# Attention of a two-layer encoder on one core: TensorE issues in source order, and a slot's products run in two halves around its P·V and its transpositions

## The chip, the core and the metric

The kernel runs on 1 core of one Trainium2 chip. The time is the device time of one execution in microseconds (us), and lower is better. Before the change the median of 3 runs is 2469.16 us (2467.95 to 2470.55).

A core has five engines with a queue each: TensorE (PE in the profile: matrix products and transpositions; PEld is its weight loading), VectorE (DVE), ScalarE (ACT), GpSimd (POOL), and SyncE (SP), which here only issues DMAs. The program holds a list of instructions for each engine, and in the trace an engine's instructions start in the order of its list; semaphores hold an instruction back until what it reads is there and what it overwrites has been read.

## What is computed

Two layers, 1040 positions (16 meta tokens and 1024 frames), width 1024. Each layer has a group of gated linear attention heads, a group of 8 heads of softmax attention with a forget-gate bias (the part that the change is about), an output projection and a feed-forward block with a short convolution. The softmax attention, cut to what matters:

```python
c = jnp.cumsum(log_f.astype(jnp.float32), axis=1)
...
logits = jnp.einsum('bqhd,bkhd->bhqk', q_b, kf) + c_b[..., None] - c_k[:, :, None, :]
logits = jnp.where(key_pos[None, :] <= q_pos[:, None], logits, -jnp.inf)
return jnp.einsum('bhqk,bkhd->bqhd', jax.nn.softmax(logits, axis=-1), vf)
```

## The kernel before

Matrix products are done in three terms: each operand is split into a rounded part and a rest (`hi` and `lo` of the weights, `xh` and `xl` of the activations), and `mm3` (L261 to L263) issues hi·xh, lo·xh and hi·xl into one PSUM bank. The split of a weight tile is a ScalarE copy and a subtraction (on GpSimd inside the attention, on VectorE once `self.mixing` is set, in the last part of it).

The softmax attention of a layer is `fox`. Its work is cut into 72 steps: 4 pairs of heads (p), in each pair the query tiles in groups (7,8), (5,6), (3,4), (1,2), (0), in each group the two heads (e), and in each head the one or two tiles of the group (ti, the later tile first). Loop turn n of `fox` is called slot n here; there are 72 + 8 slots, and the last 8 only finish what earlier ones began. For step n, with tile i:

- **Scores**, in slot n (`fox_scores`): 1 to 3 parts of up to 464 keys (3 parts for i = 8 only, 2 for i = 4 to 7, 1 for i < 4). For each part two products into a PSUM bank of the kind `S` (L720 and L721; there are three such banks), then on VectorE the bias and the row minimum (L723, from part to part), then on ScalarE the exponential (L735), which needs the minimum over all parts, writes the tile `P` and frees the bank. There are five `P` buffers (`P_BUFS`); the third part has buffers of its own (`Ps`).
- **T**, in slot n+2 (`fox_transposes`): `P` is transposed in blocks of 116 on TensorE (L756, and L749 for the third part), into one of two banks of the kind `tr`, and for the third part into an `S` bank; a ScalarE copy and a VectorE subtraction split it into `PT` (L377, L378).
- **av**, in slot n+3 of a head's last tile (`fox_av`): P·V for the tiles of the group (L782), into the one bank `av`, then a ScalarE copy to `avs` (L785).
- **fold** and **store**, 4 and 6 slots after the group's last step: transpositions of the result and of its normalised form (L795, L821), both through an `S` bank, with a chain of small VectorE and ScalarE operations between them.

Beside this each slot gets **fill**: `Work.run` takes products of other stages from a queue that `plan` fills. From slots 4, 22 and 40 it holds the q, k and v products of the next pair of heads and then the gate products (`gr_products`: three units of 24 products, each with 6 VectorE and 3 ScalarE operations behind it); from slot 58 the last gate products; from slot 62 the first four tiles of the output projection, whose operands are split on ScalarE and VectorE at that time (`ml`, `mh`). In slots 0 to 3 the queue is empty. Before the change a slot lists av and T of the first part, the scores (at a higher priority), a portion of fill, store, fold, and then av, T and a portion of fill for each further part.

All this is source order. The engines' orders are made from it by a list scheduler, which knows the dependences, reckons with durations of its own and may draw an instruction ahead of earlier ones that would wait; TensorE's order in the attention is its work too. In the feed-forward block TensorE is under `manual_schedule`: there it issues in the order of the source.

## Time and profile before

| what | value |
|---|---|
| median of 3 runs | 2469.16 us |
| the profiled execution's own time | 2467.24 us |
| its span, first to last instruction | 2465.5 us |
| granted TensorE clock, mean | 0.999 |
| TensorE busy | 2437.9 us (99%) |
| VectorE, ScalarE, GpSimd busy | 1876.9 us (76%), 1318.9 us (53%), 384.6 us (16%) |
| softmax attention of layer 0, first score to last store | 166.2 to 500.6 us |
| the same of layer 1 | 1390.5 to 1725.0 us |

A span of 2465.5 us with TensorE busy for 99% of it leaves 27.6 us of idle TensorE. The sum hides two things: matmuls overlap in the profile, so that a busy TensorE is not one at its peak, and the other engines' shares are means over stages that differ much. The two attention stretches are 334.4 and 334.5 us long, 27% of the span together. The profiled execution's own time is 1.74 us above its span and 1.92 us below the median of the three runs.

### The profile page before, as it was taken

To read this page: it belongs to the slowest core of one execution; us is meant where nothing else is said; L and a number is where in the kernel's file an instruction comes from. 1 tells how busy PE (TensorE), PEld (TensorE's weight loads), DVE (VectorE), ACT (ScalarE), POOL (GpSimd) and SP (SyncE) were. 2 spreads that over 40 slices of the span, in tenths; PEclk is the share of its full clock that TensorE was granted. 3 is DMA by queue.
4 is the path that set the end of the run, shared out by engine and by line. 5 is a ranking of instruction groups with operands and counts; after the bars stand their busy time and mean duration, and the time that the engine had idled before them with its cause. 6 is when DMAs were issued, how large, how long until landed. Compare 5 with 4: busy or idle time off the path is not lost.

```text
span 2465.5 us, 47317 instructions
## 1 busy us (share of the span) xinstructions
PE 2437.9 (99%) x18286; PEld 2356.3 (96%) x18286; DVE 1876.9 (76%) x3769; ACT 1318.9 (53%) x2857; POOL 384.6 (16%) x565
## 2 busy tenths in 40 slices
PE   9999999999999999999999999999999999999998
PEld 8999999999999999999999999999999999997887
DVE  8666777769988888865966666777799888887567
ACT  7346666646555555642643566665465555556433
POOL 2023433210000000100210234331100000001002
PEclk9999999999999999999999999999999999999999
DMA  4222224343322214863312222243423212247822
GB/s 135 70 84 76 59 84 132 120 133 95 121 82 74 91 66 144 198 169 124 125 41 73 76 81 74 65 149 106 153 81 108 91 65 91 94 153 172 214 68 88
DMA packets 121680, 260.39 MB, mean 106 GB/s; under 512 B 15248, under 2 KB 37008, under 8 KB 121456
## 3 DMA queue, kind: packets, MB, share of 16 engines
q1 hardware_dynamic: 96864, 182.05, 23.9%
q0 software_dynamic: 22288, 72.81, 10.6%
q8 instruction: 143, 2.34, 0.4%
q10 hardware_dynamic: 2304, 2.52, 0.3%
q14 instruction: 81, 0.66, 0.1%
HBM read 176.74 MB, written 67.80 MB: 99 GB/s over the span
## 4 chain that ended last, share of the span: by engine, by line
PE 68%; issue 16%; DVE 10%; ACT 4%; DMA 1%; POOL 0%; SPq 0%; DVEq 0%; POOLq 0%; ACTq 0%
PE mm L261 8%; PE mm L263 8%; PE mm L262 8%; PE up L262 5%; PE up L263 5%; PE up L261 5%; PE down L262 5%; PE down L263 5%; PE down L261 5%; PE av L782 3%; PE tr L756 2%; PE S L720 1%; DVE S L723 1%; PE S L721 1%; ACT P L735 1%
## 5 line engine op out<-in xcount | busy, mean ns | idle before, releaser
L262 PE MATMUL up<-x,lo 128*128 128x260 f32 x2240 | 631.7, 282 | 1.0 <-DVE lo L1166 1.0
L261 PE MATMUL up<-x,hi 128*128 128x260 f32 x2240 | 631.9, 282 | 0.1
L263 PE MATMUL up<-x,hi 128*128 128x260 f32 x2240 | 631.6, 282 | 0.0
L262 PEld LDWEIGHTS up<-x,lo 128*128 128x128 f32 x2240 | 422.0, 188 | 1.5 <-DVE lo L1166 1.4
L261 PEld LDWEIGHTS up<-x,hi 128*128 128x128 f32 x2240 | 421.7, 188 | 0.4 <-ACT hi L1165 0.3
L263 PEld LDWEIGHTS up<-x,hi 128*128 128x128 f32 x2240 | 421.8, 188 | 0.0
L1165 ACT CAST hi<-raw 128x512 fp32r<-128x512 f32 (+1 forms) x490 | 266.5, 553 | 207.6 <-PE up L263 88.7
L261 PE MATMUL mm<-xh,hi 128*128 128x348 f32 (+6 forms) x1056 | 359.8, 341 | 0.0
L1166 DVE TENSOR_TENSOR lo<-raw,hi 128x512 fp32r<-128x512 f32 (+1 forms) x490 | 288.0, 603 | 79.7 <-ACT hi L1165 79.1
L263 PE MATMUL mm<-xl,hi 128*128 128x348 f32 (+6 forms) x1056 | 339.6, 322 | 0.0
L262 PE MATMUL mm<-xh,lo 128*128 128x348 f32 (+6 forms) x1056 | 338.6, 321 | 0.0
L261 PEld LDWEIGHTS mm<-xh,hi 128*128 128x128 f32 x1056 | 199.4, 189 | 2.3 <-issue 1.4
L262 PEld LDWEIGHTS mm<-xh,lo 128*128 128x128 f32 x1056 | 199.4, 189 | 0.3
L263 PEld LDWEIGHTS mm<-xl,hi 128*128 128x128 f32 x1056 | 198.6, 188 | 0.1
L1147 DVE TENSOR_TENSOR raw<-raw,raw 128x512 f32<-128x512 f32 (+1 forms) x230 | 147.5, 651 | 29.8 <-DMA raw<-in_wd_dram 27.5
L735 ACT ACTIVATE P<-S,m 116x460 f32<-116x460 f32 (+2 forms) x224 | 125.1, 562 | 77.5 <-DVE m L723 74.5
L228 ACT CAST hi<-raw 128x512 fp32r<-128x512 f32 (+2 forms) x152 | 87.4, 576 | 139.6 <-PE mm L263 56.2
L262 PE MATMUL down<-x,lo 128*128 128x260 f32 (+1 forms) x504 | 161.2, 320 | 0.2 <-DVE lo L1166 0.2
L263 PE MATMUL down<-x,hi 128*128 128x260 f32 (+1 forms) x504 | 161.0, 320 | 0.0
L261 PE MATMUL down<-x,hi 128*128 128x260 f32 (+1 forms) x504 | 161.0, 319 | 0.0
L378 DVE TENSOR_TENSOR PT<-tr,PT 116x464 fp32r<-116x464 f32 (+3 forms) x240 | 123.3, 516 | 48.9 <-ACT PT L377 47.2
L1427 POOL DMA_DIRECT2D actd<-cv x44 | 23.6, 537 | 734.6 <-DVE cv L1426 734.6
(313 smaller groups left out, 5957.4 us busy)
## 6 DMA issues: line engine op xcount, KB each, us to landing
raw<-in_wm_dram SPq DMA_DIRECT2D x326, 256.0 KB, 3.1
raw<-in_wd_dram SPq DMA_DIRECT2D x48, 256.0 KB, 4.2
actd<-cv POOLq DMA_DIRECT2D x22, 520.0 KB, 3.0
actd<-cv POOLq DMA_DIRECT2D x22, 512.0 KB, 3.0
cb<-cd SPq DMA_DIRECT2D x16, 520.0 KB, 3.8
kA<-kA SPq DMA_DIRECT2D x24, 260.0 KB, 4.1
kL<-kL SPq DMA_DIRECT2D x24, 260.0 KB, 4.7
st<-actd SPq DMA_DIRECT2D x24, 260.0 KB, 3.8
```

The source lines that it names most:

```text
L228: nc.scalar.copy(hi[:, :n, :], raw[:, :n, :])
L261: nc.tensor.matmul(ps, wh, xh[:, c0:c0 + n], start=first, stop=False, skip_group_check=more)
L262: nc.tensor.matmul(ps, wl, xh[:, c0:c0 + n], start=False, stop=False, skip_group_check=more)
L263: nc.tensor.matmul(ps, wh, xl[:, c0:c0 + n], start=False, stop=last, skip_group_check=more)
L378: nc.vector.tensor_tensor(out=lo, in0=src, in1=hi.bitcast(F32), op=ALU.subtract)
L720: nc.tensor.matmul(S[:rows, :n], q["qA"][e][:, qs], q["kA"][e][:, c0:k1], start=True, stop=False)
L735: nc.scalar.activation(P[:rows, :n], S[:rows, :n], AF.Exp, scale=-1.0, bias=m[:rows, nch - 1:nch], accum_out=(den if nch == 1 else d3[:row ...
L756: nc.tensor.transpose(tr[:w, 3 - j, :rows], P[:rows, o:o + w], id_)
L782: nc.tensor.matmul(av[:, a:b], w.rearrange("p a b -> p (a b)"), x, start=(t == ts[0] and part == 0 and i == 0), stop=(t == last and i == 1))
L1147: nc.vector.tensor_tensor(out=q[out][:, :nk, :], in0=q[a][:, :nk, :], in1=q[b][:, :nk, :], op=op)
L1165: nc.scalar.copy(hi[:, :nk, :], src[:, :nk, :])
L1166: nc.vector.tensor_tensor(out=lo[:, :nk, :], in0=src[:, :nk, :], in1=hi[:, :nk, :].bitcast(F32), op=ALU.subtract)
```

## The change

TensorE is put under `manual_schedule` for the whole of `fox`, so that it issues what the source lists in the order of the source. The other engines are still ordered by the scheduler. The order within a slot is rewritten: scores, half of the slot's fill, av of all parts, T of all parts, fold, store, the other half of the fill.

```diff
@@ fox, the loop over slots
             fill_us = work.left / max(starts[p_next] - n, 1)
-            for kind in ('av0', 'T0'):
-                run(n, kind)
             if n < len(steps):
...
                 self.fox_schedule(lyr, at, n, p, e, ti, i, tiles, Ps, st, qs[p], ap, pp, mix3)
-            parts = [c for c in "12" if (n, "av" + c) in due or (n, "T" + c) in due]
-            work.run(fill_us / (1 + len(parts)))
-            run(n, "store")
-            run(n, "fold")
-            for c in parts:
-                run(n, "av" + c)
-                run(n, "T" + c)
-                work.run(fill_us / (1 + len(parts)))
+            work.run(fill_us / 2)
+            for kind in ("av0", "av1", "av2", "T0", "T1", "T2", "fold", "store"):
+                run(n, kind)
+            work.run(fill_us / 2)
@@ attention
-                self.fox(lyr, ap, pp, qs, plan, lambda: box["mix"][KD - 1])
+                with tc.manual_schedule(engines={mybir.EngineType.PE}):
+                    self.fox(lyr, ap, pp, qs, plan, lambda: box["mix"][KD - 1])
```

No product, transposition or DMA is added or removed. Over a layer's stretch from the first score to the last store TensorE goes over from one kind of work to another (products, scores, av, transpositions) 713 times before and 330 times after in layer 0, and 692 and 330 times in layer 1; it enters a run of transpositions 208 times before and 80 times after in layer 0.

The order on TensorE at the start of a layer's attention, before: behind the scores of slot 0 stand eighteen products of the fill (`mm`), of which the last is the first row here, then the scores of slot 1 (`S` with `kA_1594`), the first of slot 2 (`kA_1595`, the other head), and T of slot 0's step among them.

```order
L263 MATMUL mm<-xl_146,hi 128x344
L720 MATMUL S<-kA_1594,qA_1592 116x460
L721 MATMUL S<-kL_1596,qA_1592 116x460
L756 MATMUL tr<-ident,P 116x116 x2
L720 MATMUL S<-kA_1594,qA_1592 116x464
L721 MATMUL S<-kL_1596,qA_1592 116x464
L720 MATMUL S<-kA_1595,qA_1593 116x460
L721 MATMUL S<-kL_1597,qA_1593 116x460
L756 MATMUL tr<-ident,P 116x116 x6
L261 MATMUL mm<-xh_147,hi 128x344
L262 MATMUL mm<-xh_147,lo 128x344
L263 MATMUL mm<-xl_148,hi 128x344
```

The same place after: the first row is the first score of slot 1, which stands right behind those of slot 0.

```order
L720 MATMUL S<-kA_1594,qA_1592 116x460
L721 MATMUL S<-kL_1596,qA_1592 116x460
L720 MATMUL S<-kA_1594,qA_1592 116x464
L721 MATMUL S<-kL_1596,qA_1592 116x464
L720 MATMUL S<-kA_1595,qA_1593 116x460
L721 MATMUL S<-kL_1597,qA_1593 116x460
L720 MATMUL S<-kA_1595,qA_1593 116x464
L721 MATMUL S<-kL_1597,qA_1593 116x464
L720 MATMUL S<-kA_1595,qA_1593 116x116
L721 MATMUL S<-kL_1597,qA_1593 116x116
L756 MATMUL tr<-ident,P 116x116 x8
L749 MATMUL tr<-ident,Ps 116x116
```

What moved: the products are gone from between the scores of slots 0 to 3; the first now stand behind the scores of slot 4. T of a step stands in one run behind all scores of its slot.

The order on TensorE in slot 20, before: scores of the second head's tile 8 (three parts), with av of tile 0 of the pair before (`PT_3267`) and T of slot 18's step among them.

```order
L795 MATMUL fo<-ident,avs 116x128 x4
L782 MATMUL av<-PT_3267,V_1599 128x112
L720 MATMUL S<-kA_2327,qA_2325 116x460
L782 MATMUL av<-PT_3267,V_1599 128x112
L721 MATMUL S<-kL_2329,qA_2325 116x460
L756 MATMUL tr<-ident,P 116x116
L720 MATMUL S<-kA_2327,qA_2325 116x464
L756 MATMUL tr<-ident,P 116x116
L721 MATMUL S<-kL_2329,qA_2325 116x464
L756 MATMUL tr<-ident,P 116x116 x2
L720 MATMUL S<-kA_2327,qA_2325 116x116
L721 MATMUL S<-kL_2329,qA_2325 116x116
```

The same slot after, from the last products before its scores to the second product behind them; nine products stand between these scores and the slot's av, T and T of the third part (`Ps`).

```order
L262 MATMUL mm<-xh_143,lo 128x348
L263 MATMUL mm<-xl_144,hi 128x348
L720 MATMUL S<-kA_2329,qA_2327 116x460
L721 MATMUL S<-kL_2331,qA_2327 116x460
L720 MATMUL S<-kA_2329,qA_2327 116x464
L721 MATMUL S<-kL_2331,qA_2327 116x464
L720 MATMUL S<-kA_2329,qA_2327 116x116
L721 MATMUL S<-kL_2331,qA_2327 116x116
L261 MATMUL mm<-xh_145,hi 128x348
L262 MATMUL mm<-xh_145,lo 128x348
```

What moved: before, another kind of work stands between the scores of most parts; after, the three parts come at once, and whatever one of them waits for holds all that is listed behind it.

The order on VectorE from slot 19's first score part to slot 20's, after (`L687` to `L691` are the gate operations of the fill, `den` the sum of a row's exponentials, `ff` the copy that frees the fold's bank):

```order
L687 TENSOR_TENSOR gog<-gx,gog 128x344
L378 TENSOR_TENSOR V_2333<-tr,V_2333 116x2x64
L723 ISA S,m<-S,cb,m 116x464
L723 ISA m 116x1
L378 TENSOR_TENSOR Vm<-tr,Vm 116x64
L688 SCALAR_TENSOR_TENSOR ge<-ge,gy 128x344
L378 TENSOR_TENSOR PT_3295<-tr,PT_3295 112x112
L689 SCALAR_TENSOR_TENSOR gy<-ge,gy 128x344
L691 SCALAR_TENSOR_TENSOR gog<-gy,gog 128x344
L739 TENSOR_REDUCE den<-d_3273 116x1
L799 TENSOR_TENSOR ff<-fo,ff 116x256
L723 ISA S,m<-S,cb 116x460
```

Before, the same operations stand here in nearly the same order; VectorE's list changes little, and what changes is when TensorE delivers to it.

## The prediction, made before the changed kernel was run

> **What bounds the kernel now.** I read the page first, then windows over the two attention stretches, then the timelines of TensorE, ScalarE and VectorE at the places where the windows show idle TensorE. The page's span and TensorE's row:
>
> ```profile
> span 2465.5 us, 47317 instructions
> PE 2437.9 (99%) x18286; PEld 2356.3 (96%) x18286; DVE 1876.9 (76%) x3769; ACT 1318.9 (53%) x2857; POOL 384.6 (16%) x565
> ```
>
> TensorE bounds the kernel. The change moves work on TensorE alone, within the softmax attention, so the question is how much idle it removes there or makes. The windows (microseconds busy per engine, instructions in brackets) are the start of layer 0's attention, the scores of tiles 8 and 7 of the second and of the fourth pair of heads, and the turn to the output projection:
>
> ```profile
> core 0: us, PE busy (x) PEld busy (x) DVE busy (x) ACT busy (x) POOL busy (x), PEclk, DMA share, GB/s
> 166.00:186.00 20.00, 18.64 (x120) 15.61 (x119) 14.69 (x49) 13.93 (x43) 5.30 (x8) 1.00 0.15 46
> 245.00:265.00 20.00, 19.68 (x137) 18.12 (x136) 19.11 (x63) 15.88 (x50) 6.44 (x9) 1.00 0.22 69
> 405.00:425.00 20.00, 19.57 (x131) 17.87 (x130) 18.14 (x63) 17.29 (x55) 5.12 (x10) 1.00 0.34 118
> 445.00:463.00 18.00, 14.88 (x112) 13.79 (x111) 17.86 (x54) 14.88 (x43) 5.74 (x11) 1.00 0.48 136
> ```
>
> The reader should see VectorE: busy for 19.11 of 20 us and 18.14 of 20 us in the tile-8 zones and 17.86 of 18 us at the turn. TensorE keeps up there only because what it is given next is mostly ready. An order that makes VectorE idle in these zones lengthens them. At the start neither VectorE nor ScalarE is full, but TensorE has fill to do: rows of its timeline there (start, duration, line, shape, count).
>
> ```profile
> 167.62 0.21 PE L720 MATMUL S<-kA,qA 128*116 128x116 f32 x1
> 167.68 0.26 PE L721 MATMUL S<-kL,qA 128*116 128x116 f32 x1
> 167.78 0.38 PE L261 MATMUL mm<-xh,hi 128*128 128x344 f32 x1
> 167.99 0.32 PE L262 MATMUL mm<-xh,lo 128*128 128x344 f32 x1
> 168.15 0.32 PE L263 MATMUL mm<-xl,hi 128*128 128x344 f32 x1
> ...
> 170.77 0.47 PE L720 MATMUL S<-kA,qA 128*116 128x460 f32 x1
> ...
> 182.18 0.40 PE L782 MATMUL av<-PT,V 116*128 116x256 f32 x2
> 182.42 0.56 PE L756 MATMUL tr<-ident,P 116*116 116x116 f32 x4
> 182.74 0.41 PE L782 MATMUL av<-PT,Vm 116*128 116x116 f32 x2
> ...
> 184.46 0.26 PE L756 MATMUL tr<-ident,P 116*116 116x116 f32 x1
> 184.48 0.36 PE L720 MATMUL S<-kA,qA 128*116 128x232 f32 x1
> 184.68 0.27 PE L721 MATMUL S<-kL,qA 128*116 128x232 f32 x1
> 184.78 0.32 PE L263 MATMUL mm<-xl,hi 128*128 128x348 f32 x1
> ```
>
> **Part 1, fewer changes of kind: a saving.** What counts is the distance between starts. The lone transposition at 184.46 gives way after 0.02 us, but the score behind it then takes 0.20 instead of the 0.10 of its twin at 184.68: 0.12 together, and the four at 182.42 cost 0.08 each plus about 0.1 once behind them, 0.10 to 0.11 each. A run thus costs some 0.013 us of its own, and 128 of 208 runs per layer go: 1.7 us. The narrow score at 167.62 leaves after 0.06 since its twin uses the same weights; the twin leaves after 0.10, and the product behind it after 0.21 instead of 0.16: 0.1 us lost where a narrow matmul meets other weights. I count about 78 such places per layer in the order before and 51 after: at most 3 us. The saving is 1.7 to 4.8 us per layer; some of the narrow ones cost only half, so I take 4.0. Parts 2 to 4 compare whole stretches, which have their share of it within them, 92 of a layer's 334.4 us; outside them 2.9 us are left, with the ends 1.7 and 3.5.
>
> **Part 2, the start: a loss.** Slots 0 to 3 have no fill, and it now stays behind slot 4's scores. ScalarE and VectorE rows there:
>
> ```profile
> 169.99 0.64 ACT L735 ACTIVATE P<-S,m 116x460 f32<-116x460 f32 x1 [0.21 <-DVE m L723]
> ...
> 170.71 0.66 ACT L735 ACTIVATE P<-S,m 116x464 f32<-116x464 f32 x1
> ...
> 172.85 0.55 ACT L377 CAST PT<-tr 116x464 fp32r<-116x464 f32 x1 [1.04 <-PE tr L756]
> ```
>
> ```profile
> 171.49 0.65 DVE L723 CUSTOM_DVE_ANT_0 S<-S,cb 116x460 f32<-116x460 f32 x1 [0.41 <-PE S L721]
> ...
> 172.37 0.71 DVE L723 CUSTOM_DVE_ANT_0 S<-S,cb,m 116x464 f32<-116x464 f32 x1 [0.17 <-DVE den L739]
> ...
> 173.59 0.64 DVE L378 TENSOR_TENSOR PT<-tr,PT 116x464 fp32r<-116x464 f32 x1
> ```
>
> Three S banks carry all scores, so slot 1's first part waits for the exponential of slot 0's, done at 170.6: before, eighteen products fill 167.78 to 170.77, and after, TensorE stands for 2.99 us. From there I follow the new order with these durations (a minimum 0.65 to 0.75, an exponential 0.65, a cast of PT 0.55, its subtraction 0.64, a wide score pair 0.42). Slot 2's second part needs slot 1's exponentials, which begin after its second minimum at 172.9: it starts at 173.6 (1.4 us idle), its third at 174.2. T of slot 0 runs to 175.1; its third block needs the bank of slot 2's first part, whose minimum ends at 175.0 and exponential at 176.0 (0.95 idle). Slot 3's scores wait for slot 2's further exponentials (0.6), T of slot 1 for the casts and subtractions of the T before it (0.6), slot 4's second part for slot 3's exponential, queued on ScalarE behind two casts, until 179.8 (0.8). At 180.2 the fill begins; some 7.4 us were idle. Before, TensorE had finished slot 5's scores at 184.78. After, it still owes at 180.2 the 32 products done by then (at 0.157, 5.0 us), av of the first pair of tiles (16 at 0.12 and two narrow ones, 2.1 us), 13 transpositions (1.3) and slot 5's scores (0.6): 189.2. The loss is 4.4 us per layer; 3.4 if ScalarE's list takes an exponential before a cast at one place more, 5.4 if each hop between engines costs 0.1 us more than I reckon.
>
> A page of the Trainium skill speaks against this change here: "TensorE: Matmul & The Clock Gate", section "Part 1: The HAM clock gate", says that after an idle window of about 3.4 us the array's clock falls to half until it has been busy for as long. No run here shows it: the granted clock is 1.00 in every window above. By the page the sum would hardly change for 2.99 us of idle, and the rival below prices the other case.
>
> **Part 3, three zones per layer: a loss.** Slots 18 to 21, 36 to 39 and 54 to 57 hold tiles 8 and 7 and, at the same time, the gate units with their six VectorE operations each. Rows of VectorE in the first zone (gate, `den`, slot 19's first part, the end of the gate chain, slot 20's first part) and of TensorE (first scores of slots 18, 20 and 22):
>
> ```profile
> 242.41 0.52 DVE L680 TENSOR_TENSOR gx<-mm,r 128x344 f32<-128x344 f32 x1 [0.80 <-PE mm L263]
> 243.38 0.16 DVE L739 TENSOR_REDUCE den<-d 116x1 f32<-116x3 f32 x1 [0.45 <-ACT Ps L735]
> ...
> 244.32 0.64 DVE L723 CUSTOM_DVE_ANT_0 S<-S,cb 116x460 f32<-116x460 f32 x1
> ...
> 247.25 0.50 DVE L691 SCALAR_TENSOR_TENSOR gog<-gy,gog 128x344 f32<-128x344 f32 x1
> ...
> 248.11 0.64 DVE L723 CUSTOM_DVE_ANT_0 S<-S,cb 116x460 f32<-116x460 f32 x1
> ```
>
> ```profile
> 238.64 0.42 PE L720 MATMUL S<-kA,qA 128*116 128x460 f32 x1
> ...
> 246.78 0.47 PE L720 MATMUL S<-kA,qA 128*116 128x460 f32 x1
> ...
> 257.95 0.38 PE L720 MATMUL S<-kA,qA 128*116 128x460 f32 x1
> ```
>
> Before, slots 18 to 22 take 19.3 us. In the new order I count from slot 18's first score. TensorE reaches slot 20 after 8.35 us; but VectorE, idle from 2.5 to 4.3 us until slot 18's exponentials let `den` pass, takes slot 19's second minimum only at 7.5 to 8.3, the exponential that frees the bank ends at 9.15, and the third bank (the fold's) is read by VectorE until 10.55: 1.45 us idle, as the three parts now stand in one block. T's third block, listed behind slot 20's av and T, waits 0.55 for slot 20's first exponential (13.7). That is 2.0 us. In slot 21 the two T wait 0.6 each for the tr banks, since the subtractions stand behind gate operations on VectorE, the fold 0.25 for the bank of T's third block, and the store 1.2 for slot 21's exponential, whose second minimum is last in VectorE's row: 2.65 more, if all stand. Slot 22 then begins at 22.5, or at 19.85 with slot 20's waits alone. Before it began at 19.3 with 0.7 us of its av done, so at 18.6 for the same work. The zone costs 1.25 to 3.9 us more. The idle of slot 20 itself gives VectorE time to catch up, so I take a third of slot 21's part (0.9): some 2.2, times three, 6.6 per layer, ends 3.75 and 11.7.
>
> **Part 4, the turn to the output projection.** What it waits for there (us in total over both layers, times, longest):
>
> ```profile
> PE tr L756 <- DVE PT L378: 3.7, 5, 1.4
> PE mm L263 <- DVE ml L378: 2.1, 2, 1.0
> ```
>
> VectorE is full either way. The wait of 1.0 for `ml` goes, because av and T now stand ahead of those products. In its place the second unit waits for its weights' subtraction, 2.1 us by VectorE's list, and later av waits some 2 us for PT behind seven splits of `ml`, where before nine further products covered it. Against TensorE's 3.1 us of idle in this window I take 1.0 us more per layer, ends 0 and 2.
>
> DMAs keep their places: each is issued by SP or GpSimd, whose lists follow the scheduler as before, and none stands on TensorE's waits above except weights fetched a tile ahead. Outside these places every operand of a slot is made one or two slots earlier (334.4 / 80 = 4.2 us each), which covers a cast and a subtraction (1.2 us) and two minima with their exponentials (2.7 us); without that cover each part of scores would cost its chain.
>
> **The sum.** Per layer −2.9 + 4.4 + 6.6 + 1.0 = +9.1 us, for two layers +18.2. Against the profiled execution's own time of 2467.24 that is 2485.4; against the median of 2469.16, 1.92 higher, 2487.4. The low ends give −3.5 + 3.4 + 3.75 + 0 = +3.65 per layer, 2476.5; the high ends −1.7 + 5.4 + 11.7 + 2 = +17.4, 2504.0.
>
> **Rivals.**
> - *The banks are free in time, and the regrouping pays: faster.* Scores that come in one block give VectorE its minima earlier. If each exponential then ends before its bank is wanted, the zones keep no wait at all (slot 22 at 17.85 instead of 18.6, −0.75 each), the turn costs nothing, and of the start only the empty slots' first 2.99 us and the 1.4 us behind them stay, 4.4 of its 7.4 us idle, a loss of 1.4: −2.9 + 1.4 − 2.25 = −3.75 per layer, 2461.7. For it: ScalarE has 4 us of room in the zone. Against it: VectorE's 19.11 of 20. It decides at exponentials 0.8 us earlier than mine in slot 19.
> - *The start alone costs:* the zones' and the turn's waits vanish, the start stays at 4.4: −2.9 + 4.4 − 2.25 = −0.75 per layer, 2467.7, no change that can be told. Zones at 0.9 us each and the turn at 0 give +4.2 per layer; between these, up to +2.4 per layer, lies the case "same".
> - *TensorE is slow for a while after the start's idle.* At half speed the 5.0 us of its work in slots 1 to 4 take 5.0 more, of which the waits there hide all but some 1.7 us: +3.4 for both layers, 2490.8. The Trainium skill's page cited in part 2 has this rule. For it: 7.4 of 12.4 us idle, with 2.99 in one piece; against it: a longest idle of 1.4 us is all that before shows, at clock 1.00.
>
> **How the numbers follow.** Forecast 0.67, the clock's case 0.05, the start alone 0.17, the regrouping pays 0.11. The forecast's own range is 2474 to 2504; to hold 8 in 10 I let the range begin at 2469, within the case of no change, and end at 2503. No change means within 0.2% (4.9 us), about what a measurement of this kernel can tell: slower 0.72, same 0.17, faster 0.11.
>
> **What would show it.** In the profile after: at both starts a first score idle by about 3 us behind ACT P, and TensorE busy some 13 of 20 us; in each zone idle before L720 and L749 behind ACT P and before L756 behind DVE PT, VectorE below its 19.11; an attention stretch longer by 9 us per layer; feed-forward stretches unchanged. I would be wrong if the zones' waits are absent (2.5 us or less per layer), or if waits appear in slots 6 to 17, which I hold covered.

## The result: slower by 46 us, two and a half times the forecast

| | before | after |
|---|---|---|
| median of six runs | 2469.69 us (2467.95 to 2471.59) | 2515.68 us (2510.45 to 2520.04) |
| ratio | | 1.0183, 95% interval 1.0173 to 1.0194 |
| span of the profiled execution | 2465.5 us | 2511.6 us |
| softmax attention of layer 0, first score to last store | 334.4 us | 352.0 us (166.80 to 518.75) |
| the same of layer 1 | 334.5 us | 359.7 us (1411.72 to 1771.43) |

The sign was forecast; the size (+18.2, range to 2503) was not. The two stretches are longer by 17.6 and 25.2 us, 42.8 of the 46.1 us between the two spans. Of the other 3.3 us, 3.1 lie between the two stretches; about 1 us of that is products that moved out of the first one (below), and the rest is not explained here.

The page after the change: span, TensorE's row, and the clock in 40 slices.

```profile
span 2511.6 us, 47351 instructions
PE 2453.9 (98%) x18286; PEld 2366.3 (94%) x18286; DVE 1885.7 (75%) x3769; ACT 1320.8 (53%) x2857; POOL 386.9 (15%) x565
...
PEclk9999999999999999999999899999999999999999
```

The same 18,286 matmuls make TensorE "busy" for 16.0 us more than before, and one slice of the clock has an 8: some of the busy time is slow time. The windows (columns as before: busy us per engine, PEclk is the granted clock) of the start, two zones and the turn of layer 0, and the start and third zone of layer 1:

```profile
166.00:186.00 20.00, 14.63 (x65) 10.80 (x64) 12.45 (x42) 10.83 (x34) 3.42 (x6) 0.74 0.17 50
248.00:269.00 21.00, 18.06 (x115) 15.63 (x114) 16.95 (x57) 14.74 (x49) 5.44 (x9) 1.00 0.21 67
418.00:439.00 21.00, 17.14 (x110) 14.77 (x109) 16.00 (x55) 15.64 (x51) 5.44 (x12) 1.00 0.45 148
460.00:478.00 18.00, 13.58 (x104) 12.59 (x103) 17.89 (x50) 14.12 (x42) 5.53 (x10) 1.00 0.35 108
...
1411.00:1435.00 24.00, 18.64 (x92) 14.66 (x92) 12.53 (x43) 12.17 (x39) 3.42 (x6) 0.72 0.14 40
...
1665.00:1693.00 28.00, 22.90 (x123) 20.75 (x123) 17.96 (x62) 16.57 (x52) 6.59 (x13) 0.82 0.40 131
```

At the start TensorE starts 65 matmuls in 20 us where it started 120. In the first and third zone of layer 0 VectorE has fallen from 19.11 and 18.14 of 20 us to 16.95 and 16.00 of 21: no engine is full there any more, they wait for each other. What TensorE waits for (us over both layers, times, longest), and one row of VectorE:

```profile
PE S L720 <- ACT P L735: 15.4, 14, 3.2
PE tr L756 <- DVE PT L378: 6.7, 14, 0.8
PE tr L821 <- ACT P L735: 6.2, 6, 1.1
...
DVE S L723 <- POOL cb L894: 4.1, 2, 2.8
...
PE mm L262 <- DVE wl L230: 3.5, 2, 1.8
PE av L782 <- DVE PT L378: 3.3, 2, 1.7
...
PE mm L263 <- DVE ml L378: 2.1, 2, 1.1
```

Before, the first of these rows was:

```profile
PE S L720 <- ACT P L735: 1.9, 4, 0.6
```

and no wait ahead of the store (L821) was long enough to be listed. To see where the time went, the stretches are cut at the first scores of certain slots. From each piece's length I subtract what its matmuls take at full rate, by distances between starts in undisturbed rows: 0.417 ns per column plus 13 ns for a product, 99 ns per 116 columns for a transposition. What is left is the piece's overhead, in us; it holds waits, slow starts and, where the clock is low, the slower streaming:

| piece (slots) | before, layer 0 / 1 | after, layer 0 / 1 | difference |
|---|---|---|---|
| start (0 to 5) | 3.28 / 3.34 | 11.22 / 12.01 | +7.94 / +8.67 |
| 5 to 17 | 2.27 / 2.22 | 2.18 / 2.13 | −0.09 / −0.09 |
| first zone (17 to 22) | 2.09 / 1.81 | 5.43 / 5.41 | +3.34 / +3.60 |
| 22 to 35 | 1.93 / 2.45 | 1.25 / 1.23 | −0.68 / −1.22 |
| second zone (35 to 40) | 1.87 / 1.81 | 5.41 / 6.79 | +3.54 / +4.98 |
| 40 to 53 | 1.86 / 2.39 | 1.31 / 2.60 | −0.55 / +0.21 |
| third zone (53 to 58) | 2.32 / 2.07 | 6.29 / 11.20 | +3.97 / +9.13 |
| 58 to 62 | 0.54 / 0.84 | 0.34 / 0.37 | −0.20 / −0.47 |
| turn (62 to 67) | 4.61 / 4.57 | 5.81 / 5.79 | +1.20 / +1.22 |
| 67 to the last store | 1.08 / 1.04 | 1.25 / 1.21 | +0.17 / +0.17 |

Together +18.6 and +26.2: the starts 16.6, the six zones 28.6, the turns 2.4, and −2.8 for the rest, where the regrouping was to pay. (Some 1 us of products per layer left the stretch and stands behind its end, so that the stretches are longer by 42.8 and not by 44.8.)

### The profile page after: what moved, and what is told of

The parts are those of the page before. It is cut to its first block, busy times and chain, and to the rows that moved or that the text cites. A ratio compares the mean times of both kernels' runs of the same rounds, so it can differ in the third digit from the quotient of the medians.

```text
span 2511.6 us, 47351 instructions
## 1 busy us (share of the span) xinstructions
PE 2453.9 (98%) x18286; PEld 2366.3 (94%) x18286; DVE 1885.7 (75%) x3769; ACT 1320.8 (53%) x2857; POOL 386.9 (15%) x565
## 4 chain that ended last, share of the span: by engine, by line
PE 50%; issue 31%; DVE 12%; ACT 3%; DMA 3%; POOL 1%; SPq 0%; POOLq 0%; DVEq 0%; ACTq 0%
PE mm L261 7%; PE mm L262 7%; PE mm L263 7%; PE down L261 5%; PE down L262 5%; PE down L263 5%; PE av L782 3%; PE tr L756 2%; PE S L720 1%; PE S L721 1%; DVE S L723 1%; DVE x L1186 1%; PE wo L263 1%; PE wo L262 1%; PE wo L261 1%
## 5 line engine op out<-in xcount | busy, mean ns | idle before, releaser
L378 DVE TENSOR_TENSOR PT<-tr,PT 116x464 fp32r<-116x464 f32 (+3 forms) x240 | 117.5, 514 | 65.3 <-ACT PT L377 64.5
```

The lines of the kernel that those rows point to most:

```text
L378: nc.vector.tensor_tensor(out=lo, in0=src, in1=hi.bitcast(F32), op=ALU.subtract)
```

## The experiments

### Which part of the change costs

The new source order alone, without `manual_schedule`:

```diff
-                with tc.manual_schedule(engines={mybir.EngineType.PE}):
-                    self.fox(lyr, ap, pp, qs, plan, lambda: box["mix"][KD - 1])
+                self.fox(lyr, ap, pp, qs, plan, lambda: box["mix"][KD - 1])
```

> One part of the change alone: the new source order within a slot, with TensorE's order left to the list scheduler. Theory: the loss comes from TensorE being held to the source's order at places where the scheduler would have drawn products forward (slots 0 to 3, and the zones of tiles 8 and 7). Then this kernel is near the one before: 2465 to 2478, no window of granted clock 0.50 in the attention, TensorE idle at the starts no more than the kernel before. Rival: the regrouping itself costs, whoever orders TensorE; then 2495 or more.

2479.21 us, ratio to before 1.0024 to 1.0054. (Each group of runs has its own median of the kernel before, 2468.7 to 2469.4 us, and the ratios go by that.) The starts (3.12 and 4.59, of which 1.2 us in layer 1 is a wait for a DMA) and zones (1.71 to 2.43) are those of the kernel before or near; what it loses, it loses in the quiet slots (4.04 and 3.04 in 22 to 35, 4.02 and 3.06 in 40 to 53), where scores wait for exponentials. It is 1.2 us over the upper end of the expectation, and one window of 3.41 us at clock 0.50 stands at layer 1's turn, where none was expected.

`manual_schedule` alone, with the old order within a slot:

```diff
-                self.fox(lyr, ap, pp, qs, plan, lambda: box["mix"][KD - 1])
+                with tc.manual_schedule(engines={mybir.EngineType.PE}):
+                    self.fox(lyr, ap, pp, qs, plan, lambda: box["mix"][KD - 1])
```

> The other part alone: TensorE in source order, with the old source order within a slot (av and T of the first part, scores, fill, store, fold, av and T of further parts with fill between). Theory: the start stays as bad as in the changed kernel (slots 0 to 3 hold no products, 8 us per layer, clock at 0.50 there), but the zones lose less since products stand between the runs of transpositions: 2480 to 2500. Rival: the old order, made for a scheduler, waits in every slot once it is held, since av and T stand ahead of the scores: over 2515.

2491.93 us, 1.0077 to 1.0107, as expected: starts 9.24 and 10.00, zones 2.77 to 3.97, and turns 8.24 and 5.87, in layer 0 with 6.83 us at clock 0.50. So the parts cost 9.8 and 22.6 us alone and 46.0 together. Holding TensorE to the source costs the start with either order; the zones' large waits need both parts.

### The start: missing fill, and a clock that matters less than it shows

The products of the next pair queued from slot 0:

```diff
-        starts = [f + 4 for f in first] + [first[3] + 8, len(steps) + 8]
+        starts = [0] + [f + 4 for f in first[1:]] + [first[3] + 8, len(steps) + 8]
```

> The changed kernel with the products of the next pair queued from slot 0 instead of slot 4, so that slots 0 to 3 have fill. By the trace of the changed kernel the stretch from slot 0 to slot 5 costs 7.9 us in layer 0 and 8.7 us in layer 1 more than before. Theory: all of it is the missing fill (waits and, behind them, the clock at 0.50 for 10.2 and 13.7 us), so 2515.7 - 16.6 = 2499, within 2496 to 2503, and clock 1.00 at both starts. Rival: only the waits that the prediction counted go (4.4 us per layer) and the rest moves to slots 4 to 17, whose fill gets thinner: 2505 to 2510.

2499.59 us, 1.0106 to 1.0140; 16.1 less than the changed kernel, as expected. Starts 4.30 and 3.50, clock 1.00:

```profile
166.00:190.00 24.00, 21.67 (x142) 19.38 (x141) 13.49 (x44) 13.97 (x43) 8.38 (x11) 1.00 0.13 40
```

The changed kernel has 98 matmuls in this window and a clock of 0.79 (its row stands below). Is the clock the cause or a companion? Two kernels add products that nobody reads, where TensorE waits:

```diff
+    def keep(self, pp, q, n):
+        ps = pp.tile([128, 512], F32, tag="mm", name="keep")
+        for i in range(n):
+            self.nc.tensor.matmul(ps[:, :348], q["qA"][0][:, 0:128], q["kA"][0][:, 0:348], start=i == 0, stop=i == n - 1)
...
+            if n in (0, 1, 2, 3):
+                self.keep(pp, qs[0], 8)
             work.run(fill_us / 2)
             for kind in ("av0", "av1", "av2", "T0", "T1", "T2", "fold", "store"):
                 run(n, kind)
+                if n in (21, 39, 57) and kind in ("T1", "fold"):
+                    self.keep(pp, qs[p], 3)
```

> The changed kernel with extra products whose result is never read, put where TensorE waits: eight of 348 columns behind the scores of slots 0 to 3, and three behind the transpositions and behind the fold of slots 21, 39 and 57. They change no wait of the work itself; they only keep TensorE active. Clock theory: the clock falls to 0.50 at the end of a 3.41 us window in which TensorE streams less than about 1 us (transpositions counted half). Then it stays at 1.00 at both starts and in the zones, except perhaps ahead of slot 56 of layer 1, where TensorE waits 3.2 us with nothing added. In the changed kernel some 24 us of streaming lie in the slow windows, which at full speed take 12 less: 2503 to 2509 with the waits unchanged, so that the waits are the larger part of the loss. Rival: the low clock only fills time in which TensorE would have waited anyway: 2513 to 2520.

2507.90 us, 1.0141 to 1.0172: 7.8 less. Both starts are at clock 1.00, yet slot 5 begins 22.8 and 22.3 us after the first score, against 23.2 and 24.0 (17.7 and 17.8 before). The start of layer 1:

```profile
1411.00:1435.00 24.00, 21.65 (x136) 18.57 (x137) 14.50 (x50) 12.35 (x41) 3.47 (x7) 1.00 0.11 37
```

One fall was left, in slot 56 of layer 1, and one came at that layer's turn. Since in slots 2 and 3 the eight products might take more time than the waits there, the second kernel has 8, 5, 2 and 2 of them:

```diff
+                self.keep(pp, qs[0], (8, 5, 2, 2)[n])
```

> The changed kernel with extra products whose result is never read, as before in the zones (three behind the transpositions and three behind the fold of slots 21, 39 and 57), and fewer at the start: 8, 5, 2 and 2 behind the scores of slots 0 to 3, which is what fits into the waits of 2.9, 1.3 and 0.5 us there; with eight in each slot they stood in the way themselves (1.3 us of them in slots 2 and 3 were not covered). Theory: the clock stays at 1.00 and slot 5 begins 20.5 to 21.5 us after the first score instead of 23.2 and 24.0 (17.7 before the change): about 2.5 us per layer are the clock's, 3 to 4 the waits'. The total: 2503 to 2506. Rival: the chain of minima, exponentials, casts and subtractions alone makes 22.5 us or more: 2506 to 2509.

2508.96 us, 1.0143 to 1.0171. In layer 0 the clock holds (in layer 1 it fell for 6.8 us at the start once more), and slot 5 begins 22.9 us after the first score. The rival holds. The windows of this kernel and of the changed one:

```profile
166.00:190.00 24.00, 18.97 (x116) 15.25 (x115) 13.39 (x45) 12.84 (x40) 3.42 (x6) 1.00 0.14 42
```

```profile
166.00:190.00 24.00, 18.63 (x98) 14.80 (x97) 13.19 (x45) 12.87 (x40) 3.42 (x6) 0.79 0.14 42
```

The same row but for the extra products and the clock. The second product of the first scores waited 0.56 us longer for a DMA here than in the changed kernel (0.68 against 0.12), so the clock is worth 0.3 to 0.9 us in layer 0. In layer 1 keep_all begins slot 5 1.74 us earlier, but the changed kernel also waits 0.42 us longer there for the same DMA, so that 1.3 to 1.7 us are the clock's. At half speed TensorE mostly fills time in which it would have waited for ScalarE and VectorE.

### The zones: four waits in one run

All that follow but the last are built on the kernel with fill from slot 0. The table gives their zones' overheads in us, first, second and third of each layer; the names are those of the experiments below. The times are medians, the overheads those of the profiled execution. For fill from slot 0 this one took 2495.57 us, 4.0 less than the median of its four, so that gains against its row come out low; in it the clock fell for 3.41 us in each zone of layer 1.

| kernel | us | layer 0 | layer 1 |
|---|---|---|---|
| before | 2469.7 | 2.09, 1.87, 2.32 | 1.81, 1.81, 2.07 |
| fill from slot 0 | 2499.6 | 6.14, 5.40, 6.66 | 7.10, 6.76, 8.95 |
| mid_fill | 2492.8 | 6.97, 3.65, 6.65 | 8.03, 3.43, 6.74 |
| gate_light | 2488.2 | 6.11, 3.97, 6.55 | 6.11, 4.00, 9.07 |
| gate_moved | 2508.9 | 7.18, 8.83, 7.11 | 8.46, 8.79, 7.02 |
| cb_act | 2496.0 | 7.26, 6.69, 5.08 | 6.17, 6.78, 5.44 |
| store_av | 2494.6 | 6.16, 4.18, 6.01 | 7.34, 4.16, 6.49 |
| t0_first | 2492.0 | 4.48, 3.99, 4.79 | 4.42, 3.97, 4.68 |
| old_fill_manual | 2481.6 | 4.34, 2.80, 3.12 | 4.36, 2.87, 3.82 |

Slot 21 of the changed kernel on TensorE (start, duration, shape, count; in brackets the idle time ahead and what ended it):

```profile
263.03 0.32 PE L263 MATMUL mm<-xl,hi 128*128 128x348 f32 x1
263.82 0.58 PE L756 MATMUL tr<-ident,P 116*116 116x116 f32 x4 [0.47 <-DVE PT L378]
264.80 0.58 PE L756 MATMUL tr<-ident,P 116*116 116x116 f32 x4 [0.40 <-DVE PT L378]
265.85 0.43 PE L795 MATMUL fo<-ident,avs 128*112 128x128 f32 x2 [0.47 <-DVE PT L378]
267.30 0.42 PE L821 MATMUL tr<-ident,fon 116*128 116x116 f32 x2 [1.01 <-ACT P L735]
267.48 0.41 PE L261 MATMUL mm<-xh,hi 128*128 128x348 f32 x1
```

and on VectorE in the same time:

```profile
262.03 0.65 DVE L723 CUSTOM_DVE_ANT_0 S<-S,cb 116x460 f32<-116x460 f32 x1 [1.10 <-PE S L721]
...
262.60 0.52 DVE L688 SCALAR_TENSOR_TENSOR ge<-ge,gy 128x348 f32<-128x348 f32 x1
263.04 0.63 DVE L378 TENSOR_TENSOR PT<-tr,PT 116x464 fp32r<-116x464 f32 x1
263.59 0.51 DVE L689 SCALAR_TENSOR_TENSOR gy<-ge,gy 128x348 f32<-128x348 f32 x1
264.02 0.63 DVE L378 TENSOR_TENSOR PT<-tr,PT 116x464 fp32r<-116x464 f32 x1
264.57 1.04 DVE L691 SCALAR_TENSOR_TENSOR gog<-gy,gog 128x348 f32<-128x348 f32 x1
265.53 0.27 DVE L378 TENSOR_TENSOR PT<-tr,PT 116x116 fp32r<-116x116 f32 x1
265.72 0.69 DVE L723 CUSTOM_DVE_ANT_0 S<-S,cb,m 116x464 f32<-116x464 f32 x1
```

Four groups of transpositions wait in a row, 2.35 us, with nothing between them. VectorE, idle until the slot's first scores come, then takes gate operations and subtractions in turn, and the slot's second minimum last; the exponential that frees the store's S bank comes behind that minimum. In the kernel with fill from slot 0 the second and third zones wait in the same way; in the first zones the two T wait 1.8 us, and the store does not.

A third of the fill between T and fold:

```diff
-            work.run(fill_us / 2)
-            for kind in ("av0", "av1", "av2", "T0", "T1", "T2", "fold", "store"):
-                run(n, kind)
-            work.run(fill_us / 2)
+            work.run(fill_us / 3)
+            for kind in ("av0", "av1", "av2", "T0", "T1", "T2"):
+                run(n, kind)
+            work.run(fill_us / 3)
+            for kind in ("fold", "store"):
+                run(n, kind)
+            work.run(fill_us / 3)
```

> On top of the kernel with fill from slot 0 (2499.6): the fill of a slot in thirds, scores, a third, av and T, a third, fold and store, a third. What is left of the loss there lies in the three zones of a layer (slots 17 to 22, 35 to 40, 53 to 58), 11.9 us in layer 0 and 17.1 us in layer 1 above the kernel before. Theory: the store of slot 21 (1.0 us behind the exponential of the same slot's scores) and the fold wait because they stand right behind the transpositions; five products ahead of them cover 0.8 of it, and no window without products is left, so the clock stays at 1.00: 6 times 1.2 and some 3 for the clock, 2487 to 2493. Rival: the waits are VectorE's backlog and only move to the next slot: 2497 to 2501.

2492.75 us, 1.0080 to 1.0110, within the range, but not in the way expected: the second zones gain 1.8 and 3.3, the first lose 0.8 and 0.9, slots 22 to 35 lose 1.2 and 0.5, and the store still waits 6.3 us in all. The clock fell seven times in the attention.

Two of the gate's VectorE operations left out:

```diff
-            nc.vector.scalar_tensor_tensor(out=e, in0=e, scalar=1.0, in1=y, op0=ALU.add, op1=ALU.mult)
-            nc.vector.scalar_tensor_tensor(out=y, in0=e, scalar=-2.0, in1=y, op0=ALU.add, op1=ALU.mult)
```

> On top of the kernel with fill from slot 0: two of the gate's six VectorE operations are left out (L688 and L689, so the gate's value is another one); the products, the DMAs and ScalarE's part stay. Theory of the prediction (step 3): in slot 21 the subtractions of PT and the second minimum stand behind the gate's operations on VectorE, 0.5 us each, so the zone's waits shrink by 0.5 to 1.0 us: 6 zones, 2493 to 2497. Rival: the waits are the chain transposition, cast, subtraction, bank itself, whatever VectorE does beside it: 2498 to 2501.

2488.22 us, 1.0063 to 1.0097: 11.4 less, more than expected, 3.6 of it at the turns (3.93 and 4.03 instead of 5.77 and 5.81), where gate operations also stand. TensorE's wait for PT ahead of T falls from 7.1 us (13 times) to 1.4 (3 times), but the store's rises from 4.2 to 6.7 us, and the scores' wait for the fold's bank (`ff`) from 0.4 to 3.4: the first wait of the row is shortened and later ones take much of it back. Only the second zones (1.4 and 2.8 us) and the first of layer 1 (1.0) gain, and in these two of layer 1 a fall of the clock is gone as well.

The gate's products moved ahead of the v products:

```diff
                         self.gr_products(lyr, p, w, ap, pp, nm)
+                        w.q[6:] = w.q[9:] + w.q[6:9]
+                        w.boxes[2:] = w.boxes[:1:-1]
@@ fox
             work.run(fill_us / 2)
+            if n in starts[1:4]:
+                self.flush()
             for kind in ("av0", "av1", "av2", "T0", "T1", "T2", "fold", "store"):
```

> On top of the kernel with fill from slot 0: in the first three plans the gate's products are queued behind the k products instead of behind the v products, so that the gate's VectorE work lies in slots 12 to 17 (light tiles) and the v products, with about half of that work, in the zone. All of the computation stays. Theory: the zones wait since the gate's operations stand on VectorE among those of tiles 8 and 7; then the zones lose some 2 us less each and the clock does not fall: 2483 to 2491. Rival: av of slot 22 then waits for V (its last products now end there), and the zone only changes its wait: 2496 to 2504.

2508.93 us, 1.0146 to 1.0176: 9.3 worse than its base, against both expectations. Slot 21 has no wait now, as the theory says of the gate, in any of the six zones, but the v products' own transpositions take the `tr` banks of the zone:

```profile
255.60 0.58 PE L756 MATMUL tr<-ident,P 116*116 116x116 f32 x4 [1.94 <-DVE V L378]
...
258.88 0.96 PE L756 MATMUL tr<-ident,P 116*116 116x116 f32 x8
259.68 0.38 PE L795 MATMUL fo<-ident,avs 128*112 128x128 f32 x2
260.18 0.42 PE L821 MATMUL tr<-ident,fon 116*128 116x116 f32 x2
```

The third zone has one more cause, which the prediction had excluded. Rows of layer 0, changed kernel, by engine (SPq is SyncE's queue):

```profile
409.38 0.33 SPq L869 DMA_DIRECT2D cb<-cd  x1
417.06 0.34 SPq L219 DMA_DIRECT2D raw<-in_wm_dram  x1
417.44 0.42 SPq L869 DMA_DIRECT2D cb<-cd  x1
```

```profile
415.74 1.29 POOL L230 TENSOR_TENSOR lo<-raw,hi 128x512 fp32r<-128x512 f32 x1
...
423.80 0.82 POOL L894 TENSOR_TENSOR cb<-cb,mask 116x116 f32<-116x116 f32 x2 [5.17 <-DMA cb<-cd]
```

```profile
424.66 0.71 DVE L723 CUSTOM_DVE_ANT_0 S<-S,cb,m 116x464 f32<-116x464 f32 x1 [1.23 <-POOL cb L894]
```

```profile
426.25 0.47 PE L720 MATMUL S<-kA,qA 128*116 128x460 f32 x1 [1.87 <-ACT P L735]
```

The new order of the other engines' lists put a weight DMA between the bias rows (`cb`) of a pair's two heads on SyncE. It waits for its buffer, which GpSimd's split of an earlier tile frees at 417.03, and the second row comes 8.06 us after the first (2.32 before the change; over the six zones 5.6 to 8.1 against 2.3 to 3.6). GpSimd, in its own order, waits for that row ahead of a mask that the first head needs, VectorE for the mask, ScalarE and TensorE behind it. In layer 1 TensorE waits 3.18 us there. First try, the mask written later in the source:

```diff
-                        self.fox_mask(cbs[p][x], NT - 1)
+                if g == 0 and ti == 1:
+                    self.fox_mask(cbs[p][e], NT - 1)
```

> On top of the kernel with fill from slot 0: the first mask on the second head's bias row (cb) is written in the source at the second head's first scores (slot 20, 38, 56) instead of the first head's (slot 18, 36, 54). In the changed kernel the DMA of that row stands on SyncE behind a weight DMA and comes 4.9 to 7.6 us after the first row's (0.4 to 3.6 us before the change's kernel), and GpSimd, in its own order, waits for it ahead of the first head's next mask; in the third zone VectorE's minimum of slot 55 then waits 1.2 us in layer 0 and 2.8 us in layer 1 for that mask, and TensorE's scores of slot 56 1.9 and 3.2 us. Theory: without that order the wait ahead of slot 56 shrinks to the 0.5 us of the other zones, 1.3 and 2.6 us less and one clock window less: 2494 to 2497. Rival: the row itself is late for the second head, and the wait moves to slot 56: 2498 to 2501.

2498.39 us, 1.0105 to 1.0136. VectorE still waits 3.7 us for the mask: the scheduler placed GpSimd's masks as before, and the run tells nothing on the cause. (The delays of the row quoted in its expectation were misread; those above are the rows'.) Second try, the second row through another queue:

```diff
-                        nc.sync.dma_start(cbs[p][x][:, :T],
+                        (nc.scalar if x else nc.sync).dma_start(cbs[p][x][:, :T],
```

> On top of the kernel with fill from slot 0 (2499.6): the bias row (cb) of a pair's second head is fetched through ScalarE's queue, so that it no longer stands behind a waiting weight DMA on SyncE. Writing its mask later in the source (the run before) left GpSimd's order as it was and told nothing. Theory: the 1.2 and 2.2 to 2.8 us that VectorE's minimum in the third zone waits for GpSimd's mask go, and with them 1.3 us of the zone in layer 0 and 2.5 to 4 us in layer 1 (a window of the clock too): 2494 to 2496. Rival: the wait there is VectorE's own backlog and stays: 2498 to 2501.

2495.99 us, 1.0092 to 1.0126: VectorE's wait for the mask is gone from the list, the third zones lose 1.6 and 3.5 us less, as expected. In the first two zones of layer 0 the clock fell instead, 1.1 and 1.3 us.

The store in the bank of av:

```diff
-        tr = pp.tile([128, 4, 128], F32, tag="S", name="tr")
-        trf = tr[:].rearrange("p a b -> p (a b)")
+        trf = pp.tile([128, 256], F32, tag="av", name="tr")
```

> On top of the kernel with fill from slot 0 (2499.6): the store's transpositions go to the bank of av (no av stands in slots 21, 39 and 57) instead of an S bank. Theory: of the zone's waits the store's 1.0 to 1.1 us in slot 21 is that for an S bank, behind an exponential whose minimum is last in VectorE's row; it goes in four to six zones, and a clock window or two with it: 2492 to 2496. Rival: fold and store are also late by their own chain, or av of the next slot waits for the store's bank: 2498 to 2501.

2494.60 us, 1.0080 to 1.0110. The store follows the fold without a wait:

```profile
1585.50 0.43 PE L795 MATMUL fo<-ident,avs 128*112 128x128 f32 x2 [0.47 <-DVE PT L378]
1585.77 0.36 PE L820 MATMUL tr<-ident,fon 116*128 116x116 f32 x2
```

The second and third zones gain 6.9 us together (in the first the store had no wait in this base); the turns lose 4.8, where av now waits for the store's bank, and layer 0's start lost 2.4 more, with a wait of 1.9 us for a DMA and a fall of the clock. So the store's wait is one for the bank.

T and av of the first part ahead of the scores, all else new:

```diff
+            for kind in ("av0", "T0"):
+                run(n, kind)
             if n < len(steps):
...
-            for kind in ("av0", "av1", "av2", "T0", "T1", "T2", "fold", "store"):
+            for kind in ("av1", "av2", "T1", "T2", "fold", "store"):
```

> On top of the kernel with fill from slot 0 (2499.6): in a slot, av and T of the first part stand ahead of the scores, as the kernel before lists them; all else keeps the new order. What is left of the loss is in the zones, 4.0, 3.5, 4.3 us in layer 0 and 5.3, 5.0, 6.9 us in layer 1 above the kernel before; with TensorE in the old order these were 0.7, 0.9, 0.8 and 1.1, 1.0, 1.9. Theory: two T of a slot right behind each other need both tr banks at once, and each waits for the other's cast and subtraction; with the scores and half of the fill (2.6 us) between them the wait goes: 2482 to 2490. Rival: the store, which waits 1.0 us for an S bank, is the larger part, or a T ahead of the scores only delays these: 2495 or more.

2492.02 us, 1.0079 to 1.0109, between the two expectations. All six zones shrink, by 1.4 to 4.3 us, and no clock falls in them. The waits for PT are gone from slots 21, 39 and 57, as the theory says; what is left in the zones are T's third block (1.3 to 1.4 us) and the store (1.0 to 1.2). But slots 22 to 35 (2.78) and the turns (8.72 and 8.63 instead of 5.8, with 6.83 us at clock 0.50 in each) give about half of it back.

The old order held, with fill from slot 0 (the kernel of the second run with the one line that gave the changed kernel its fill):

```diff
-        starts = [f + 4 for f in first] + [first[3] + 8, len(steps) + 8]
+        starts = [0] + [f + 4 for f in first[1:]] + [first[3] + 8, len(steps) + 8]
```

> TensorE in source order, the old order within a slot, and fill from slot 0. The kernel with the old order held (2491.9) loses 6.0 and 6.7 us more than the kernel before from slot 0 to slot 5, 4 us in its zones and 3.6 and 1.3 us at the turn to the output projection. Theory: fill at the start takes away 5 to 6.5 us per layer as it did with the new order (6.9 and 8.5), the rest stays: 2479 to 2483. Rival: T ahead of the scores waits for its P at the start whatever fill there is: 2486 or more.

2481.55 us, 1.0033 to 1.0063, as expected. The difference to the same with the new order, 18 us, is what the new order costs once TensorE is held: zones of 5.4 to 9.0 instead of 2.8 to 4.4, while the old order loses 2.8 us more at the turns.

### Is there a version that gains?

Fill from slot 0 in the kernel before, by the same line:

```diff
+        starts = [0] + [f + 4 for f in first[1:]] + [first[3] + 8, len(steps) + 8]
```

> The kernel before (2469.3) with fill from slot 0 and nothing else; the list scheduler orders TensorE. Theory: the scheduler drew products forward into slots 0 to 3 anyway (2.2 us of lag there beyond that of other slots), so at most 1 us per layer is to be had: 2467 to 2470. Rival: the fill of slots 4 to 17 gets thinner and the scores wait there: 2471 to 2476.

2469.42 us, 0.9991 to 1.0010: no change. The starts have 1.5 and 1.7 us less overhead, and slots 17 to 35 have 2.0 and 1.5 more.

That kernel with TensorE held in the new order in the quiet slots only:

```diff
+        quiet = {*range(6, 17), *range(23, 35), *range(41, 53), *range(59, 62)}
+            if n in quiet and n - 1 not in quiet:
+                held.enter_context(self.tc.manual_schedule(engines={mybir.EngineType.PE}))
...
+            if n in quiet:
+                work.run(fill_us / 2)
+                for kind in ("av0", "av1", "av2", "T0", "T1", "T2", "fold", "store"):
+                    run(n, kind)
+                work.run(fill_us / 2)
+                if n + 1 not in quiet:
+                    held.close()
+                continue
```

> The kernel before with fill from slot 0 (2469.4), where TensorE is held to the source's order and a slot has the changed order only in slots 6 to 16, 23 to 34, 41 to 52 and 59 to 61, where no zone, start or turn stands; the scheduler keeps the rest. By the traces the changed order loses 1.6, 1.3 and 1.3 us to overheads in slots 5 to 17, 22 to 35 and 40 to 53, against 2.3, 1.9 and 1.9 us (layer 0) and 2.2, 2.5 and 2.4 us (layer 1) before. Theory: the regrouping pays there, 1.5 to 2.5 us per layer: 2464 to 2467, the fastest of all. Rival: at the borders of the held stretches the scheduler's list comes out worse, and the gain is lost: 2468 to 2473.

2473.12 us, 1.0005 to 1.0023, 3.7 us above its base, at the rival's upper end. Slots 5 to 17 take 1.18 us of overhead (1.79 and 1.31 in its base), but the pieces at the borders take it back (17 to 22: 3.63 and 3.62 instead of 2.68 and 2.48), and layer 0 loses 1.7 us in slots 22 to 35, where the clock falls once, and 1.5 in its third zone. No version beat the kernel before.

## Why the prediction had the sign and not the size

The parts sum to 44.8 us where +18.2 was forecast. Of the 26.6 us between, the zones make 15.4 (28.6 against 13.2), the starts 7.8 (16.6 against 8.8), the saving 3.0 (2.8 against 5.8) and the turns 0.4. So two steps failed: the discount of slot 21's waits in step 3, with the low clock and the late bias row that the zones' sum did not have at all, and the length of the chain in step 2.

**Step 1, the saving: right in kind, half the size.** −2.9 per layer outside parts 2 to 4 was forecast; the pieces outside give −1.4 (layer 0: −0.09 − 0.68 − 0.55 − 0.20 + 0.17) and −1.4 (layer 1). In 40 to 53 of layer 0 the saving is 0.55; slots 5 to 17, where a wait of 0.8 for PT (at 211 and 1457 us) stands against it, saved nothing. The prediction had held those slots covered. No run tells why the other pieces fell short. The prediction's low end of this term was also misworked: the share that turns 4.0 into 2.9 and 4.8 into 3.5 turns 1.7 into 1.2, so that −1.4 lies within its own ends.

**Step 2, the start: the first hops right, the chain too short.** The first piece was to stand 2.99 us, and the distance from the last score of slot 0 to the first of slot 1 is 2.89; the 1.4 us behind it are 1.29. Then the working and the rows part:

```profile
171.70 0.47 PE L720 MATMUL S<-kA,qA 128*116 128x460 f32 x1 [2.62 <-ACT P L735]
...
174.88 0.74 PE L720 MATMUL S<-kA,qA 128*116 128x464 f32 x1 [1.29 <-ACT P L735]
...
178.36 0.45 PE L749 MATMUL tr<-ident,Ps 116*116 116x116 f32 x1 [0.50 <-ACT P L735]
...
184.17 0.32 PE L261 MATMUL mm<-xh,hi 128*128 128x344 f32 x1
```

Counted from the first score, slot 2's second part starts at 8.1 us (7.4 forecast), T's third block at 11.6 (9.8), the fill at 17.4 (14.0). The loss of 7.94 and 8.67 instead of 4.4 is this term, mis-sized, and its high end of 5.4 too. With the clock at 1.00 it starts at 17.1 (keep_thin, 0.6 of it a DMA's), so it is the chain of waits that was reckoned too short: it lags the forecast by 0.4 us at slot 1's first score and by 0.7, 1.8 and 3.4 at the three places. Minima, exponentials, casts and subtractions queue on two engines, and the high end had allowed 0.1 us more for each hop. No run prices the single hops.

**The rival of the slow clock, given 0.05, came true and cost less at the start than its price.** The clock fell at both starts, for 10.24 and 13.65 us, and cost 0.3 to 0.9 and 1.3 to 1.7 us, against 3.4 in all. What the rival lacked is that it falls in the zones of layer 1 too: 6.8, 6.8 and 3.4 us at half speed there, and keep_all, which keeps the clock up in all but one zone, is 7.8 us faster in all. In layer 1, 2.7 us of the second zone and the slots behind it (1.38 and 1.29 more than in layer 0) are the clock's: in keep_all these two pieces are no longer than in layer 0. So is part of the third zone's 4.9 more.

**Step 3, the zones: the right waits, wrongly discounted.** If all stood, slot 22 was to begin 3.9 us late; the three zones without a fall of the clock or a wait for the bias row lose 3.3 to 3.6. Six such zones would be some 21 us, by their mean, against 13.2 forecast; the other 7.6 of the 28.6 are the low clock's and the late row's. Slot 21's waits are there as written, 0.47, 0.40, 0.47 and 1.01 against 0.6, 0.6, 0.25 and 1.2. I took a third of them, since idle in slot 20 would let VectorE catch up. It does not: VectorE idles 1.1 us for slot 21's first scores and then works off its list in the list's order, subtractions and gate ahead of the minimum. Slot 20's wait is smaller than forecast in the first two zones (0.5 of 1.45 us), and the 0.55 us of T's third block there did not come. gate_light and gate_moved show that gate operations hold slot 21's waits for PT; t0_first, that these come from two T in a row; store_av, that the last wait is for the bank.

**"DMAs keep their places" was false.** SyncE's and GpSimd's lists are made by the scheduler from the same source, and came out with a weight DMA between the two bias rows. That is 1.6 us of the third zone in layer 0 and, with the clock, 3.5 in layer 1 (cb_act). The lists of the queues could have been compared before.

**Step 4, the turn: right in size, partly by luck.** +1.2 per layer against +1.0. The wait for wl (1.8, forecast 2.1) and av's for PT (1.7, forecast 2) came, both a little shorter; the one for ml, which was to go, stayed at 1.0. These errors nearly cancel.

What I had said would show it wrong, zones of 2.5 us or less and waits in slots 6 to 17, did not happen but for the one wait above. The clock's share in the Trainium skill's terms: the page "TensorE: Matmul & The Clock Gate", section "Part 1: The HAM clock gate", which the prediction weighed as an idle window of about 3.4 us, also says there that the window runs freely, 3413 ns long. The trace agrees: all falls and rises of one execution lie on a grid of 3.413 us (10.24, 13.65, 6.83 and 3.41 us are 3, 4, 2 and 1 of them). So 2.99 us of idle in one piece was never the question; what a fixed window holds is, by the counts at the end of this document.

## What to carry to other kernels

Before an engine is held to the order of the source, list for each slot what it would stand for if nothing were drawn forward: a scheduler's value is at the slots where the source has no cover, and these are few and costly. Runs of like work have fewer changes of kind but take their banks all at once. Independent work between two runs took the waits for their banks away (t0_first), but where the engines that free the banks are busy, part of the wait moves to the next operation (gate_light, mid_fill). And compare the orders of the DMA queues as well as of the engine that was touched.

## What the runs showed of the hardware

In these runs the granted clock changes only at the ends of windows of 3.413 us, and whether it falls goes with how much TensorE streams in the window, not with one idle piece. Two windows of the changed kernel with much the same row, slot 39 (what slot 21 is in the first zone) in layer 1 and in layer 0, and the time behind the first:

```profile
1593.29:1596.70 3.41, 1.80 (x12) 0.96 (x10) 3.41 (x8) 1.87 (x6) 2.04 (x3) 1.00 0.11 14
1596.70:1603.53 6.83, 6.10 (x21) 5.96 (x22) 4.45 (x15) 3.34 (x11) 2.24 (x3) 0.50 0.29 100
347.43:350.84 3.41, 2.08 (x14) 1.24 (x12) 3.41 (x7) 1.99 (x5) 1.76 (x2) 1.00 0.01 2
```

The first holds transpositions and waits, no wait longer than 1.0 us, and the clock falls at its end; the second has two products more, and it stays (0.86 and 1.10 us of streaming by the count that follows). I counted streaming time in all windows of seventeen traces (columns at 0.417 ns, a transposition's 99 ns counted half, the window taken 0.35 us ahead of the recorded change). These two numbers are fitted; the half stands already in keep_all's expectation, on record before the other fifteen traces. Of 12,248 windows at full clock, all 19 with less than 0.7 us ended in a fall, none of the 12,140 with more than 1.4 us did, and 35 of 89 between, so that the count decides at both ends and leaves a range open. At half clock, every window with 2.3 us or more ended it and none with 2.1 or less did. The Trainium skill's page "TensorE: Matmul & The Clock Gate" says in its section "Part 4: PE-mode transpose" that transpositions do not count as busy in the same way. The first row above agrees as far as one row can: ten of its twelve matmuls are transpositions, TensorE is busy for 1.80 of 3.41 us, and the clock falls.

What a fall costs hangs on what stands behind it: 10.24 us at half speed cost 0.3 to 0.9 us at a start where TensorE waited anyway, and 6.83 us cost 2.7 in and behind the second zone of layer 1.
